# A two-layer hybrid encoder on one core: the mixer's GpSimd sums taken off GpSimd, the score scale moved from bias to q, and the v loads spread

## The chip, the core and the metric

The kernel runs on one core of one Trainium2 chip. TensorE (PE in the profile) multiplies, VectorE (DVE), ScalarE (ACT) and GpSimd (POOL) work on tiles in SBUF, and SyncE (SP) issues most of the transfers. The metric is the time of one execution in microseconds on the device. Lower is better.

## What is computed

```python
for l in range(2):
    x = x + 0.5 * swiglu(rms_norm(x, ffn1_norm[l]), ffn1_w_in[l], ffn1_w_out[l])
    x = x + mixer(rms_norm(x, mix_norm[l]), ...)
    x = x + 0.5 * swiglu(rms_norm(x, ffn2_norm[l]), ffn2_w_in[l], ffn2_w_out[l])
return rms_norm(x, final_norm)

def mixer(h, w_in, gate_bias, rpb, w_na_out, w_f_out, w_o):
    z = h @ w_in                       # q, k, v (512 each), uf (512), ga, gf (1024 each)
    y_na = neighbourhood_attention(q, k, v, rpb) @ w_na_out   # scores * 64**-0.5 + bias, softmax
    y_f = fourier_mix(uf) @ w_f_out    # real part of a 2-D DFT over positions and channels
    return (sigmoid(ga + gate_bias[0]) * y_na + sigmoid(gf + gate_bias[1]) * y_f) @ w_o
```

There are 512 positions of 1024 features in float32, 8 heads of 64, an 8 by 64 grid, and a feed-forward width of 2816.

## The kernel before

Each matrix is used as a sum of two parts, a rounded high part and the remainder, so every product takes three matmuls: high by high, high by low, low by high (`mm3`, L326 to L328; `product_T`, L515 to L517). The large products are done by a seven-product scheme on 2 by 2 blocks; its steps are numbered 1 to 7, and some take sums of weight blocks and sums of activation blocks.

All weights come through one stream, `ws`, a fixed list of items in the order of use. An item's raw tile is loaded by SyncE (L152). `high` makes `whi` on ScalarE (L186, L184 with a sign change) and `low` makes `wlo` on VectorE (L193, L191). `ws.next` prepares up to two items ahead. Sums of two weight blocks are made in two ways: by an accumulating transfer that GpSimd issues onto the raw tile (L154 when it is loaded, L203 after its low part is taken), or, for an item with `op=ALU.subtract`, by loading both blocks and a GpSimd subtraction (L166).

```python
            if self.add:
                self.add.load()
                if self.op is not ALU.add:
                    G.tensor_tensor(self.raw.t, self.raw.t, self.add.t, self.op)
```

`stage_mixer` writes out the order of its work by hand; each engine runs its own queue in order, and the scheduler keeps that order except for small moves. In order of time it does:

- `proj_V`: the v projection for four row blocks, and the even (`hp`, from `plus`) and odd (`hm`) combinations of the normalised rows for the Fourier branch. The odd one is a GpSimd subtraction (L1004). v goes to a DRAM tensor `vd` by SyncE (L974).
- `proj_U`: the Fourier input by even weights (`ue`, items "up") and odd weights (`uo`, items "um" less "un", L166).
- 14 loads of `vc` from `vd` (seven tiles, two halves each, L1410), all issued by SyncE right after `proj_U`.
- `proj_q`, `proj_k` for four head pairs, eight `att_step`s (scores, transposes and the product with `vc` are pipelined over three steps), and the position and channel transforms between them. `bias_for` loads the bias tiles `bm`; GpSimd multiplies them by 8 (L1169), and the scores take the bias with a factor of 1/8 for the whole sum (L1192).
- `f_fill`: the Fourier output rows in eight parts, with even (`pe`, items "fp" plus "fq") and odd (`po`, items "fp" less "fq", L166) products in two PSUM banks each.
- `gate_block` 0 and 1: the two gate projections by the seven products, tiles A, B and C, with sums of activation blocks made by `minus` on VectorE (`t1`) and GpSimd (`t3`, L1469, L1471) and by `fourth` on GpSimd (L1476, L1477). Between them `fill_n` multiplies the attention output by its weights.
- the output projection `w`, and the next stage's norm.

All tiles named "k" share 23 buffers of 4 KB per partition; PSUM has 8 banks used in turn.

Of the kernel before, what the change touches and what calls it, by code (L numbers as in the profile page):

```python
# [9 lines left out]
F32 = mybir.dt.float32  # L10
F32R = mybir.dt.float32r
# [83 lines left out]
def encoder_kernel(  # L95
# [60 lines left out]
    class Item:  # L156
        def __init__(self, raw, add=None, neg=False, stage=0, parts=1, pieces=1, then=None, op=ALU.add, kept=False):
            self.raw, self.add, self.neg, self.stage, self.parts = raw, add, neg, stage, parts
            self.pieces, self.then, self.op, self.kept = pieces, then, op, kept

        def load(self):
            self.raw.load(self.pieces)
            if self.add:
                self.add.load()
                if self.op is not ALU.add:
                    G.tensor_tensor(self.raw.t, self.raw.t, self.add.t, self.op)  # L166

        def high(self):
            n = self.raw.n
            if self.kept:  # L170
                self.out = (slot(F32R, "whi", (1024,))[:, 0:n], slot(F32R, "wlo", (1024,))[:, 0:n])
            else:
                self.out = tuple(
                    wp.tile([P, 1024], F32R, tag=z, name=nm(z), bufs=3)[:, 0:n] for z in ("whi", "wlo")
                )
            t = self.raw.t
            if self.add and self.op is ALU.add:
# [27 lines left out]
    def stage_items():  # L205
# [46 lines left out]
        for l in range(L):  # L252
# [8 lines left out]
            for g in range(2):  # L261
                add(Raw((s, "um", g)), Raw((s, "un", g)), op=ALU.subtract)
            for g in range(8):
                add(Raw((s, "qk", g)))
            for i in range(2):
                add(Raw((s, "fp", i), 1024, (s, "fq", i)))
                add(Raw((s, "fp", i)), Raw((s, "fq", i)), op=ALU.subtract)
            for i in range(2):
                strassen(s, lambda q: "g" + q, i, two, ORDER_0[0 : 2 - i], True)
            for g in range(2):  # L270
                add(Raw((s, "n", 0, g)))
            for i, order in ((0, (5,)), (1, (2,)), (0, (6, 7, 3, 4)), (1, (5, 6, 7, 3, 4))):
                strassen(s, lambda q: "g" + q, i, two, order, True)
                st += not i and len(order) == 1
            for g in range(2):
# [5 lines left out]
    class Stream:  # L281
# [5 lines left out]
        def fetch(self, to):  # L287
            n = len(self.items)
            while self.loaded < min(to, n) and self.items[self.loaded].stage <= self.stage:
                self.items[self.loaded].load()  # L290
                self.loaded += 1

        def high(self):
            self.fetch(self.highs + FETCH[self.stage % 2])
            self.items[self.highs].high()
            self.highs += 1
# [627 lines left out]
    def stage_mixer(l, norm, nxt):  # L924
# [29 lines left out]
        def proj_V():  # L954
# [45 lines left out]
            def plus(i):  # L1000
                a, b, t = norm.raw[i, 0], norm.raw[i, 1], folds[i]
                V.tensor_tensor(t[:, :, 1:HALF], a[:, :, 1:HALF], b[:, :, HALF - 1 : 0 : -1], ALU.add)
# [37 lines left out]
            ws.low()  # L1040
            h0, h1 = upper(norm.raw[0, 0], "hm"), upper(norm.raw[1, 0], "hm")
            for c in (0, 1):
                done(c, True)
            for c in (0, 1):
                done(c, False)
            hm.append(lower(h0, norm.raw[0, 0], "hm"))
            hm.append(lower(h1, norm.raw[1, 0], "hm"))

# [123 lines left out]
        def att_scores(i, after):  # L1172
            hp, pr = divmod(i, 2)
# [17 lines left out]
            for e, jj, c, z in quarters:  # L1191
                V.tensor_tensor_reduce(  # L1192
                    s_[e][:, c], ps[e][:, c], bms[hp][e][:, pr + jj, :], -(DH**-0.5), 3.0e38, ALU.add, ALU.min,
                    nmx[:, z : z + 1],
# [3 lines left out]
            for e, jj, c, z in quarters:  # L1198
# [3 lines left out]
                if jj:  # L1202
                    V.reciprocal(rs[:, 2 * e : 2 * e + 2], sm[:, 2 * e : 2 * e + 2])
            se = s_[0].rearrange("p (a k) -> p a k", a=2)
            V.tensor_tensor(se, se, rs[:, 0:2].unsqueeze(2).to_broadcast([P, 2, 256]), ALU.mult)
# [41 lines left out]

        def att_step(i, then=None, before=None, last=None):
            if 0 <= i - 2 < 8:
# [7 lines left out]
            if i < 8:  # L1257
                sc[i] = att_scores(i, last)

# [15 lines left out]
        def f_fill(w64):  # L1275

            for i in range(2):
                (eh, el), (oh, ol) = ws.next(0), ws.next(0)
                for cb in range(4):
                    if cb % 2 == 0:  # L1280
                        fs[i, cb // 2] = slot(F32, "fs", (2, T))
                    pe, po = bank(), bank()
                    for gp in range(2):
                        c = slice(gp * T + cb * P, gp * T + cb * P + P)
                        mm3(pe[:, 0:KC], eh[:, c], el[:, c], pf[gp][:, 0, :], pf[gp][:, 1, :], gp == 0, False)
                    c = slice(i * T + cb * P, i * T + cb * P + P)
                    PE.matmul(pe[:, 0:KC], w64[0:68, c], p64[0][0:68, 0:KC], start=False, stop=True)
                    for gp in range(2):
                        c = slice(gp * T + cb * P, gp * T + cb * P + P)
                        mm3(po[:, 0:HALF], oh[:, c], ol[:, c], qf[gp][:, 0, :], qf[gp][:, 1, :], gp == 0, gp == 1)  # L1290
                    t = tmp(s="fo")[:, 0:HALF]
                    S.activation(t, po[:, 0:HALF], AF.Copy)
                    y = fs[i, cb // 2][:, cb % 2, :]
                    S.activation(y[:, HALF : HALF + 1], pe[:, HALF : HALF + 1], AF.Copy)
                    V.tensor_tensor(y[:, 0:HALF], pe[:, 0:HALF], t, ALU.subtract)
                    V.tensor_tensor(y[:, T - 1 : HALF : -1], pe[:, 1:HALF], t[:, 1:HALF], ALU.add)
# [105 lines left out]
        vch = {}  # L1402
        for b in range(7):
            t = vch[b] = slot(F32R, "vc", (2, T))
            for z in range(2):
                src = bass.AP(
                    tensor=vd.tensor, offset=vd.offset + (b + z) * 8 * 2 * T,
                    ap=[[GW * 2 * T, ROWS], [2 * T, 8], [1, 2 * T]],
                )
                nc.sync.dma_start(out=t[64 * z : 64 * z + 64].bitcast(F32), in_=src.bitcast(F32))  # L1410
# [17 lines left out]
        bias_for(3)  # L1428
        att_step(4)
        proj_k(3)  # L1430
        ws.prep(ws.pos + 2)
        att_step(5, lambda: ws.prep(ws.pos + 3))
        f_rows = f_fill(w64)
# [3 lines left out]
        block_1 = gate_block(1, acts, ORDER_0, {}, ga1, gf1, (1, 2))  # L1437
        for _ in range(4):
            next(f_rows)
        ws.high()  # L1440
        att_step(6, ws.low)
        ws.prep(ws.pos + 3)
        for _ in range(4):
            next(f_rows)
# [49 lines left out]
        next(block)  # L1494
        *_, t3 = third
        next(block_1)
# [14 lines left out]
        ws.high()  # L1511
        h3 = high(t3, "t3")
        ws.low()
        acts[7] = low(h3, t3, "t3")
        next(block)
        next(block)
        ws.high()
        next(block)
        ws.low()
        next(block)  # L1520
        ws.high()
        next(block_1)
        ws.low()
        ws.high()
        next(block_1)
        ws.low()
        ws.high()
        next(block_1)
        next(block)
# [8 lines left out]
        written.pop().__exit__(None, None, None)  # L1538
        for _ in block:
            pass  # L1540

        m00, m01 = ga0
# [259 lines left out]
```

## Time and profile before

| | |
|---|---|
| three runs | 1938.55, 1940.87, 1946.59 us; median 1940.87 us |
| the profiled execution | 1944.28 us; its span is 1942.5 us |
| mean granted TensorE clock | 0.989 |
| busy: PE, PE weight load, DVE, ACT, POOL | 97%, 82%, 78%, 60%, 14% |
| moved | 378.91 MB, mean 195 GB/s |

The first mixer lies about between 300 and 612 us of the span, the second between 1264 and 1572 us. TensorE's order of work is fixed, so the profile is read as a list of places where TensorE waits; for each, the engine that ended the wait is followed back. The granted clock in the windows tells how fast TensorE ran after a wait.

### The profile page before, as it was taken

How to read it: one execution, taken by the hardware profiler on the slowest of the kernel's cores; microseconds unless marked ns; L12 is line 12 of the kernel's file. 1: busy time of each engine (PE TensorE's matmuls, PEld its weight loads, DVE VectorE, ACT ScalarE, POOL GpSimd, SP SyncE). 2: the span in 40 equal slices, each digit the busy share in tenths (PEclk: the TensorE clock that was granted, in tenths of full speed). 3: DMA queues.
4: the chain of work that ended last, by engine and by line, in shares of the span. 5: the costliest groups of instructions: out<-in, count | busy, mean ns of one | idle time of the engine just before them, and what ended most of it. 6: DMA issues, size and time to landing. Idle time of an engine off the chain costs nothing.

```text
span 1942.5 us, 25866 instructions
## 1 busy us (share of the span) xinstructions
PE 1886.3 (97%) x9609; PEld 1595.9 (82%) x9609; DVE 1520.5 (78%) x1864; ACT 1157.3 (60%) x1718; POOL 263.8 (14%) x242
## 2 busy tenths in 40 slices
PE   9999999989899999999999999999998999999997
PEld 7888888878898888888888888888798978888886
DVE  7777799748768866779976768997586787777898
ACT  6655666547555755566655556665575666556664
POOL 0101011311411000101000100123213110000010
PEclk9999999999999999999999999999999999999998
DMA  8776497673877467749847665967639774765593
GB/s 284 204 205 187 150 257 248 205 182 120 221 189 202 132 188 201 192 151 253 248 142 199 193 178 168 264 202 245 178 130 230 194 194 127 208 180 172 173 281 125
DMA packets 108301, 378.91 MB, mean 195 GB/s; under 512 B 12288, under 2 KB 12416, under 8 KB 108176
## 3 DMA queue, kind: packets, MB, share of 16 engines
q1 hardware_dynamic: 80096, 279.38, 40.2%
q0 software_dynamic: 27648, 97.59, 27.0%
q8 instruction: 75, 1.23, 0.2%
q14 instruction: 50, 0.41, 0.1%
q10 hardware_dynamic: 432, 0.30, 0.1%
HBM read 370.93 MB, written 6.29 MB: 194 GB/s over the span
## 4 chain that ended last, share of the span: by engine, by line
PE 64%; DVE 17%; DMA 7%; issue 5%; ACT 5%; SPq 1%; POOL 0%; DVEq 0%; ACTq 0%; POOLq 0%
PE A L326 7%; PE A L328 7%; PE A L327 7%; DMA raw<-in_wst_dram 5%; DVE wlo L193 5%; PE B L328 4%; PE B L326 4%; PE B L327 4%; PE o L327 3%; PE o L328 3%; PE o L326 3%; PE C L327 2%; PE C L328 2%; PE C L326 2%; PE tr L558 2%
## 5 line engine op out<-in xcount | busy, mean ns | idle before, releaser
L193 DVE TENSOR_TENSOR wlo<-raw,whi 128x1024 fp32r<-128x1024 f32 (+2 forms) x524 | 631.2, 1213 | 319.2 <-ACT whi L186 315.7
L186 ACT ACTIVATE whi<-raw 128x1024 fp32r<-128x1024 f32 (+2 forms) x524 | 539.0, 1034 | 468.0 <-PE A L328 116.3
L154 POOL DMA_DIRECT2D raw<-in_wst_dram x162 | 142.5, 896 | 1383.9 <-DMA raw<-in_wst_dram 894.1
L178 DVE TENSOR_TENSOR raw<-raw,raw 128x1024 f32<-128x1024 f32 (+1 forms) x128 | 151.1, 1191 | 2.5
L328 PE MATMUL A<-whi,xl 128*128 128x512 f32 x320 | 124.6, 389 | 0.0
L326 PE MATMUL A<-whi,xh 128*128 128x512 f32 x320 | 124.5, 389 | 0.0
L327 PE MATMUL A<-wlo,xh 128*128 128x512 f32 x320 | 124.5, 389 | 0.0
L184 ACT ACTIVATE whi<-raw 128x1024 fp32r<-128x1024 f32 x76 | 79.2, 1042 | 67.8 <-PE B L328 33.2
L191 DVE SCALAR_TENSOR_TENSOR wlo<-raw,whi 128x1024 fp32r<-128x1024 f32 x76 | 96.1, 1269 | 20.0 <-ACT whi L184 19.9
L535 ACT ACTIVATE sn<-A 128x512 f32<-128x512 f32 x96 | 56.5, 598 | 40.3 <-PE A L328 40.1
L327 PEld LDWEIGHTS A<-wlo,xh 128*128 128x128 f32 x320 | 60.1, 188 | 12.5
L328 PEld LDWEIGHTS A<-whi,xl 128*128 128x128 f32 x320 | 60.1, 188 | 12.4
L326 PEld LDWEIGHTS A<-whi,xh 128*128 128x128 f32 x320 | 60.1, 188 | 12.4
L326 PE MATMUL B<-whi,t1h 128*128 128x512 f32 x160 | 63.7, 398 | 0.0
L327 PE MATMUL C<-wlo,xh 128*128 128x512 f32 x160 | 62.4, 390 | 0.5 <-DVE wlo L193 0.5
L327 PE MATMUL A<-wlo,t2h 128*128 128x512 f32 x160 | 62.4, 390 | 0.4 <-DVE wlo L193 0.4
L326 PE MATMUL A<-whi,t3h 128*128 128x512 f32 x160 | 62.4, 390 | 0.2 <-ACT sn L535 0.2
L326 PE MATMUL C<-whi,xh 128*128 128x512 f32 x160 | 62.2, 390 | 0.2 <-ACT whi L186 0.2
L328 PE MATMUL B<-whi,t1l 128*128 128x512 f32 x160 | 62.4, 390 | 0.0
L327 PE MATMUL A<-wlo,t3h 128*128 128x512 f32 x160 | 62.3, 390 | 0.0
L328 PE MATMUL A<-whi,t2l 128*128 128x512 f32 x160 | 62.3, 389 | 0.0
L327 PE MATMUL B<-wlo,t1h 128*128 128x512 f32 x160 | 62.3, 389 | 0.0
(426 smaller groups left out, 5339.4 us busy)
## 6 DMA issues: line engine op xcount, KB each, us to landing
raw<-in_wst_dram SPq DMA_DIRECT2D x467, 512.0 KB
raw<-in_wst_dram POOLq DMA_DIRECT2D x172, 512.0 KB, 7.9
raw<-in_wst_dram SPq DMA_DIRECT2D x30, 256.0 KB
vc<-vd SPq DMA_DIRECT2D x28, 256.0 KB
bm<-in_near_dram SPq DMA_DIRECT2D x16, 384.0 KB
vd<-v SPq DMA_DIRECT2D x8, 512.0 KB
dft<-in_dft_dram POOLq DMA_DIRECT2D x4, 514.0 KB, 8.3
x<-in_xin_dram SPq DMA_DIRECT2D x4, 512.0 KB
```

Of the source, the lines that this page charges most:

```text
L154: G.dma_start(out=self.t, in_=wst[GRAN_AT[self.plus]][:, 0 : self.n], accum_op=ALU.add)
L178: V.tensor_tensor(t, t, self.add.t, ALU.add)
L184: S.activation(self.out[0][:, cs], self.raw.t[:, cs], AF.Copy, scale=-1.0)
L186: S.activation(self.out[0][:, cs], self.raw.t[:, cs], AF.Copy)
L191: self.last = V.scalar_tensor_tensor(lo, t, -1.0, hi.bitcast(F32), ALU.mult, ALU.subtract)
L193: self.last = V.tensor_tensor(lo, t, hi.bitcast(F32), ALU.subtract)
L326: PE.matmul(ps, lh, rh, start=start, stop=False, skip_group_check=again)
L327: PE.matmul(ps, lh, rl, start=False, stop=False, skip_group_check=again)
L328: PE.matmul(ps, ll, rh, start=False, stop=stop, skip_group_check=again)
L535: S.activation(t[:, b, :], ps[b], AF.Copy)
L558: PE.transpose(tr[:, k, b * P : (b + 1) * P], a[:, b, (q + k) * P : (q + k + 1) * P], ident)
```

## The change

- The four subtracted weight items of each layer ("um" less "un" twice, "fp" less "fq" twice) are loaded as one block, negated in place by ScalarE (`ws.negate`), and the other block is added by an accumulating transfer that GpSimd issues.
- The odd combination of rows (`less_mirror`), the block sums of `t3` and those of `fourth` are made by VectorE.
- q is scaled by 1/8 when it is split into its two parts, the low part in four pieces; the bias is used as it is loaded.
- The 14 loads of `vc` are issued in four groups (`keys`), after k 0, after q 1, after the channel transform and after k 1.
- The even and odd products of `f_fill` share one PSUM bank per part, and the first part of each four is emptied in the middle of an `att_step` (`mid`).
- Step 5 of gate block 1 is put ahead of step 4 of gate block 0, in the weight stream and on TensorE.

The diff, cut to its core:

```diff
+        def negate(self):
+            t = self.raw.t
+            S.activation(t, t, AF.Copy, scale=-1.0)
+            G.dma_start(out=t, in_=wst[GRAN_AT[self.minus]][:, 0 : self.raw.n], accum_op=ALU.add)
+            self.minus = None
...
-                add(Raw((s, "um", g)), Raw((s, "un", g)), op=ALU.subtract)
+                add(Raw((s, "un", g)), minus=(s, "um", g))
...
-                add(Raw((s, "fp", i)), Raw((s, "fq", i)), op=ALU.subtract)
+                add(Raw((s, "fq", i)), minus=(s, "fp", i))
...
-            for i, order in ((0, (5,)), (1, (2,)), (0, (6, 7, 3, 4)), (1, (5, 6, 7, 3, 4))):
+            for i, order in ((0, (5,)), (1, (2,)), (0, (6, 7, 3)), (1, (5,)), (0, (4,)), (1, (6, 7, 3, 4))):
...
-                G.tensor_tensor(a[:, :, 1:HALF], a[:, :, 1:HALF], b[:, :, HALF - 1 : 0 : -1], ALU.subtract)
+            def less_mirror(i):
+                a, b = norm.raw[i, 0], norm.raw[i, 1]
+                V.tensor_tensor(a[:, :, 1:HALF], a[:, :, 1:HALF], b[:, :, HALF - 1 : 0 : -1], ALU.subtract)
...
             ws.high()
+            ws.negate()
             some((0, 1), VG[2], False, False)
+            ws.low()
             hp.append(lower(h1, folds[1], "hp"))
-            ws.low()
+            less_mirror(0)
             ws.high()
+            ws.negate()
...
-            split(hv, lv, proj_T().rearrange("p (r j c) -> p j r c", r=ROWS, j=4))
+            ps = proj_T().rearrange("p (r j c) -> p j r c", r=ROWS, j=4)
+            S.activation(hv, ps, AF.Copy, scale=DH**-0.5)
+            for j in range(4):
+                V.scalar_tensor_tensor(
+                    lv[:, j], ps[:, j], DH**-0.5, hv[:, j].bitcast(F32), ALU.mult, ALU.subtract
+                )
...
-                G.tensor_single_scalar(res, res, DH**0.5, ALU.mult)
...
-                    pe, po = bank(), bank()
+                    ps = bank("ef")
+                    pe, po = ps[:, 0:KC], ps[:, HALF:]
...
+        def keys(*bs):
+            for b in bs:
...
         proj_k(0)
+        keys(0, 1)
         proj_q(1)
+        keys(2, 3)
         att_step(0)
         four_ch()
         bias_for(1)
+        keys(4)
         proj_k(1)
+        keys(5, 6)
...
+        ws.negate()
+        att_step(4, lambda: ws.prep(ws.pos + 2))
+        ws.negate()
+        ws.prep(ws.pos + 3)
         proj_k(3)
...
-        first, third = minus(V, B[0, 0], B[0, 1], "t1"), minus(G, B[0, 1], B[1, 1], "t3")
+        first, third = minus(V, B[0, 0], B[0, 1], "t1"), minus(V, B[0, 1], B[1, 1], "t3")
         def fourth():
-            G.tensor_tensor(t12, B[1, 0][0], t12, ALU.subtract)
-            G.tensor_tensor(t12, t12, B[1, 0][1], ALU.add)
+            V.tensor_tensor(t12, B[1, 0][0], t12, ALU.subtract)
+            V.tensor_tensor(t12, t12, B[1, 0][1], ALU.add)
```

More of the change, by code (lines that the diff above doesn't have):

```diff
@@ L291, in fetch, with negate @@
                 self.loaded += 1
+        def negate(self):
+            next(z for z in self.items[self.highs :] if z.minus).negate()
         def high(self):
             self.fetch(self.highs + FETCH[self.stage % 2])
+            assert self.items[self.highs].minus is None
             self.items[self.highs].high()
@@ L1203, in att_scores @@
                     V.reciprocal(rs[:, 2 * e : 2 * e + 2], sm[:, 2 * e : 2 * e + 2])
+                    if mid and not e:
+                        mid()
             se = s_[0].rearrange("p (a k) -> p a k", a=2)
@@ L1246, in stage_mixer, with att_step @@
         sc, pt_ = {}, {}
-        def att_step(i, then=None, before=None, last=None):
+        def att_step(i, then=None, before=None, last=None, mid=None):
             if 0 <= i - 2 < 8:
@@ L1257, in att_step @@
             if i < 8:
-                sc[i] = att_scores(i, last)
+                sc[i] = att_scores(i, last, mid)
         fs, ns = {}, {}
@@ L1437, in stage_mixer @@
         block_1 = gate_block(1, acts, ORDER_0, {}, ga1, gf1, (1, 2))
-        for _ in range(4):
+        ws.high()
+        att_step(5, ws.low, mid=lambda: next(f_rows))
+        for _ in range(3):
             next(f_rows)
         ws.high()
-        att_step(6, ws.low)
-        ws.prep(ws.pos + 3)
-        for _ in range(4):
+        att_step(6, ws.low, mid=lambda: next(f_rows))
+        ws.prep(ws.pos + 1)
+        for _ in range(3):
             next(f_rows)
@@ L1511, in stage_mixer @@
         ws.high()
-        h3 = high(t3, "t3")
         ws.low()
-        acts[7] = low(h3, t3, "t3")
+        next(third)
         next(block)
         next(block)
+        next(third)
         ws.high()
@@ L1519, in stage_mixer @@
         ws.low()
+        t3 = next(third)
         next(block)
         ws.high()
+        h3 = high(t3, "t3")
         next(block_1)
@@ L1527, in stage_mixer @@
         ws.high()
+        acts[7] = low(h3, t3, "t3")
         next(block_1)
@@ L1538, in stage_mixer @@
         written.pop().__exit__(None, None, None)
-        for _ in block:
-            pass
+        for _ in range(2):
+            next(block)
+        next(block_1)
+        next(block)
         m00, m01 = ga0
```

57 lines of the change are left out of this document (28 added, 29 removed).

## The prediction, made before the changed kernel was run

> **What bounds the kernel now.** I read the page's busy times first, then the list of waits for TensorE, then the timeline around each long wait on all engines, and last the windows with the granted clock.
>
> ```profile
> PE 1886.3 (97%) x9609; PEld 1595.9 (82%) x9609; DVE 1520.5 (78%) x1864; ACT 1157.3 (60%) x1718; POOL 263.8 (14%) x242
> ...
> PE A L517 <- DVE wlo L191: 10.4, 2, 5.2
> PE ps L326 <- DVE q L333: 9.1, 2, 6.5
> ...
> PE B L515 <- ACT whi L186: 3.3, 2, 1.7
> PE ps L326 <- ACT fs L1294: 3.2, 4, 0.9
> ...
> PE ue L327 <- DVE wlo L193: 2.9, 2, 2.5
> PE uo L327 <- DVE wlo L193: 2.5, 2, 2.4
> PE B L517 <- DVE wlo L193: 1.5, 2, 0.8
> ```
>
> TensorE is the bound at 97%, and the change leaves its instructions as they are in number (on the queues of the built kernels only one product changes its place). So the time can fall only by what TensorE waits, and by the slow clock behind a wait. The rows give total, times and longest. They all lie in the two mixers, nearly each once in either.
>
> The clock behind three of these waits, in each layer:
>
> ```profile
> 412.90:420.20 7.30, 7.29 (x25) 5.79 (x26) 4.98 (x17) 5.78 (x17) 3.32 (x2) 0.75 0.79 215
> 503.20:508.70 5.50, 5.48 (x24) 5.38 (x25) 5.46 (x8) 3.20 (x6) 1.48 (x2) 0.50 1.07 264
> 548.70:552.80 4.10, 4.10 (x22) 4.10 (x23) 4.10 (x6) 2.66 (x5) 0.00 (x0) 0.61 0.60 187
> 1373.00:1381.40 8.40, 8.36 (x24) 6.63 (x25) 5.86 (x17) 5.78 (x17) 3.31 (x2) 0.64 0.65 170
> 1464.30:1468.60 4.30, 4.24 (x22) 4.24 (x23) 4.25 (x8) 2.66 (x5) 0.64 (x1) 0.60 1.07 276
> 1509.10:1513.20 4.10, 4.10 (x23) 4.10 (x24) 4.10 (x6) 2.65 (x5) 0.00 (x0) 0.62 0.51 191
> ```
>
> Third from the end stands the granted clock. Length times what is missing to 1: behind the q wait 7.30 x 0.25 + 8.40 x 0.36 = 4.8 us; behind the A wait 5.50 x 0.50 + 4.30 x 0.40 = 4.5 us; behind the B waits 4.10 x 0.39 + 4.10 x 0.38 = 3.2 us. That is time beside the waits themselves.
>
> The Trainium skill (TensorE: Matmul & The Clock Gate, Part 1) says that the clock halves only after an idle window of about 3.4 us. By that rule only the waits of 6.5 and 5.2 us would have a slow tail, 3.0 us less would come back than I count, and the forecast below would be 1912.5. The rows differ: the B waits (1.7 us and under) and the second q wait (9.1 - 6.5 = 2.6 us) also have one. The measurement decides.
>
> **Part 1, v loads.**
>
> ```profile
> 375.46 15.63 SPq L1410 DMA_DIRECT2D vc<-vd  x14
> 392.23 20.39 SPq L152 DMA_DIRECT2D raw<-in_wst_dram  x7
> 409.95 1.06 ACT L186 ACTIVATE whi<-raw 128x1024 fp32r<-128x1024 f32 x1 [12.65 <-DMA raw<-in_wst_dram]
> 412.18 0.68 DVE L333 TENSOR_TENSOR q<-ps,q 128x512 fp32r<-128x512 f32 x1
> 412.92 0.80 PE L326 MATMUL ps<-xh,whi 128*128 128x512 f32 x1 [6.50 <-DVE q L333]
> 427.63 0.28 PE L326 MATMUL ps<-p,vc 128*128 128x256 f32 x1
> ```
>
> The wait named "q" is a late weight: 14 loads of `vc` stand on SyncE's queue before the next raw block, which lands at 409.95; ScalarE and VectorE hold the q split behind that block's whi and wlo, and TensorE needs the split's PSUM bank. In the built kernel's SyncE queue three weight blocks (qk 4 to 6) move ahead of all `vc` loads, and qk 7 and the first f block go between them. So this wait goes, 9.1 us, with its tail of 4.8: 13.9 us. What is moved late is `vc`, first read at 427.63. All 14 and the block behind them took 409.95 - 375.46 = 34.5 us; with three blocks first (SyncE spent 20.39 / 7 = 2.9 us on one) the first eight of 14 land near 375.5 + 9 + 34.5 x 8/14 = 404, an estimate, and even a first read 8.3 us (6.5 + 1.8) earlier leaves 15 us. Cost: nothing; if buffers hold the loads back by more than those 15 us, part 1 is lost, which is a rival below.
>
> **Part 2, GpSimd sums.**
>
> ```profile
> 493.39 2.48 DVE L1469 TENSOR_TENSOR t<-xl 128x1024 f32<-128x1024 f32 x1
> 494.75 3.38 POOL L1469 TENSOR_TENSOR t<-xl,xl 128x1024 f32<-128x1024 f32 x1
> 495.91 3.31 DVE L1471 TENSOR_TENSOR t<-t,t 128x1024 f32<-128x1024 f32 x1
> 497.75 0.28 PE L516 MATMUL A<-xl,whi 128*128 128x256 f32 x1
> 499.14 4.03 DVE L191 SCALAR_TENSOR_TENSOR wlo<-raw,whi 128x1024 fp32r<-128x1024 f32 x1
> 499.43 2.65 POOL L1471 TENSOR_TENSOR t<-t,t 128x1024 f32<-128x1024 f32 x1
> ...
> L193 DVE TENSOR_TENSOR wlo<-raw,whi 128x1024 fp32r<-128x1024 f32 (+2 forms) x524 | 631.2, 1213 | 319.2 <-ACT whi L186 315.7
> ...
> L333 DVE TENSOR_TENSOR xl<-xr,xh 128x1024 fp32r<-128x1024 f32 x16 | 19.6, 1223 | 4.9 <-ACT xh L332 4.5
> L1002 DVE TENSOR_TENSOR ht<-xr,xr 128x1020 f32<-128x1020 f32 x4 | 4.8, 1210 | 0.0
> L333 DVE TENSOR_TENSOR q<-ps,q 128x512 fp32r<-128x512 f32 x8 | 5.5, 686 | 1.7 <-ACT q L332 1.7
> L1192 DVE CUSTOM_DVE_ANT_0 s<-ps,bm 128x256 f32<-128x256 f32 x64 | 23.2, 419 | 0.0
> ```
>
> A VectorE operation on two SBUF blocks of 128x1024 takes 1.22 us; the three beside GpSimd's sums take 2.48, 3.31 and 4.03. At 1.22 each the wlo that TensorE waits for ends 6.2 us sooner, at 497.0, ahead of the 497.9 where it is wanted. The A wait goes: 10.4 + 4.5 = 14.9 us.
>
> What VectorE takes over per layer: two mirrors, 2 x 1.21; three sums for t3, 3 x 1.22; two for fourth, 2 x 1.22; and four q splits in four pieces. A piece is 0.29 by the line through 0.686 (512) and 0.419 (256), so a split grows by 0.46, at most by 4 x 0.419 - 0.686 = 1.0. Together 2.4 + 3.7 + 2.4 + 1.8 = 10.4 us. I cost it at nothing: what hides it is VectorE's idle time ahead of wlo, 315.7 us in the run, and on its queue t3 and fourth stand after `fill_n` among such wlo; q is read two steps later. If that cover is gone, it is 20.8 us in all.
>
> One thing is late next: the second weight block of `fill_n`. On VectorE two operations of 512 columns, two of 256, and three of 1024 with its own wlo follow on 497.0: 2 x 0.69 + 2 x 0.42 + 3 x 1.22 = 5.9, so 502.9. TensorE ends A at 497.9 + 5.50 x 0.50 = 500.6 and wants that wlo eight matmuls later, at 0.23 each (7.30 x 0.75 over 24) 502.4. A wait of 0.5, 1.0 us for both layers, between none and 3.
>
> **Part 3, odd weights by negation.**
>
> ```profile
> 356.00 3.45 SPq L152 DMA_DIRECT2D raw<-in_wst_dram  x5
> 362.92 2.86 POOL L166 TENSOR_TENSOR raw<-raw,raw 128x1024 f32<-128x1024 f32 x1 [0.44 <-DMA raw<-in_wst_dram]
> 363.48 6.82 DVE L193 TENSOR_TENSOR wlo<-raw,whi 128x780 fp32r<-128x780 f32 x3
> 366.66 0.39 PE L327 MATMUL ue<-wlo,hph 128*128 128x260 f32 x1 [2.50 <-DVE wlo L193]
> 374.51 0.28 PE L326 MATMUL uo<-whi,hmh 128*128 128x256 f32 x1
> 447.15 1.06 ACT L1273 ACTIVATE w<-r 4x1024 fp32r<-4x1024 f32 x1
> 458.53 0.28 PE L326 MATMUL ps<-pq,whi 128*128 128x256 f32 x1
> ...
> DMA to landing us min/median/max: 5.1/7.9/13.9
> ```
>
> The ue and uo waits, 2.9 + 2.5 = 5.4 us, come from wlo operations of 6.82 / 3 us beside L1004 and L166; without GpSimd the even weights are ready in time. But a chain takes the subtraction's place: load, negate (1.06), an accumulating transfer, whi (1.06), wlo (1.22). For uo: the block lands one SyncE issue (0.69) earlier than the pair at 362.92, so 362.2; negated 363.2; with a landing L later, hi and lo are ready at 365.5 + L. ue takes 374.51 - 366.66 = 7.85 us, so uo wants its low part at 366.66 - 2.50 - 0.28 + 7.85 + 0.12 = 371.9 (0.28 is the matmul before the wait, 0.12 the step from one to the next: 5.50 x 0.50 over 24). The new wait is L - 6.4: 1.5 us at the median of 7.9. For f_fill: the negation follows the copy that ends at 448.2, so it ends at 449.3; hi and lo are ready at 451.6 + L, and TensorE wants them at 458.5: L - 6.9, 1.0 us. Of both, 2.5 us a layer, 5.0 in all; at 5.1 nothing; at 13.9 7.2 us each and a slow clock. ScalarE's queue holds the next whi, the mirror's high part and the v copies behind the negation's wait for its load; they have over a microsecond. The four transfers stand on POOL's queue where it had waited for the sums. The bias scaling leaves GpSimd and no one waited for it.
>
> **Part 4, one bank, and the order of steps.** Four parts of two banks took all 8 banks, and TensorE waited for them: 3.2 us, gone. Step 5 ahead of step 4 gives block 1's transfers more room; the two loads it moves past are ahead anyway. I cost it at nothing. The B waits stay:
>
> ```profile
> 546.32 2.00 ACT L186 ACTIVATE whi<-raw 128x1024 fp32r<-128x1024 f32 x2 [5.40 <-DMA raw<-in_wst_dram]
> ```
>
> They end on a crowded accumulating transfer that the change does not touch, 3.3 + 1.5 us with 3.2 of clock: 8.0 us, at best also gone.
>
> **Sum.** 13.9 + 14.9 + 5.4 + 3.2 = 37.4 us gone; 1.0 + 5.0 us new; net 31.4. The profiled execution took 1944.28 us (span 1942.5), 0.2% over the median of the runs, 1940.87. Against its own time: 1912.9; against the median, which I forecast: **1909.5 us**.
>
> **Rivals.** *VectorE becomes the bound* (0.15): at 78% it takes 20.8 us more, all of it on the path: net 10.6, 1930.3 us. For it: its rows above follow each other without a gap from 493.39 to 503.17. Against: three of its operations there get 6.2 us back. The Trainium skill (Perfetto Trace Analysis, Optimizing Scalar/DVE Operations) speaks on this side: with VectorE saturated, handing work to GpSimd may pay; it adds that the two share a read port. The rows above bear out the second half.
>
> *The v loads only move the crowd* (0.08): another weight is late by as much, part 1 gives nothing: net 17.5, 1923.4 us. Against: the SyncE queue as built.
>
> *The sums were not what slowed VectorE* (0.07): then A, ue and uo waits stay: 37.4 - 14.9 - 5.4 = 17.1, less 3.0: 1926.8 us. Against: three slow operations, each beside a GpSimd sum.
>
> *Slower: the negation chain* (0.06): both places of a layer cost L - 6.65 and a slow clock of some 2.3 us (9.3 / 4). The gain without it, 36.4, is used up, and 9.7 us (0.5%, about what a measurement here can tell) more, when 4 x (L - 4.35) = 46.1, so from L = 15.9 us. At 17: 1940.87 - 36.4 + 50.6 = 1955 us. For it: 13.9 is the longest in this mixer. Against: the median, 7.9.
>
> **How the numbers follow.** The forecast has 0.62, and 0.02 is left for others. Low end: no chain cost and the B waits gone, 1940.87 - 37.4 - 8.0 = 1895. High end: past the VectorE rival, 1932. Faster by over 0.5% is below 1931.2: the forecast and nearly all of the first three rivals, 0.88; same 0.06, slower 0.06.
>
> **Right or wrong.** Right: TensorE's waits on q, on A's L191 and on fs are gone from the list; the windows behind them show clock 1.00; VectorE's 128x1024 operations are all near 1.22; uo and f_fill wait 1 to 2 us; the B waits stay near 4.8. Wrong: a wait of TensorE on `vc`, on a whi held by a transfer behind a negation, or on a wlo behind the new sums.

## The result

Two sets of runs agree. In the first the changed kernel's median is 1918.38 us (1917.10 to 1922.43) against 1940.47 us (1938.55 to 1946.59) before, a ratio of 0.988, 95% interval 0.986 to 0.991. In the second it is 1920.50 us (1915.30 to 1924.81) against 1938.78 us, ratio 0.992, 0.988 to 0.995. It is faster by about 1%; forecast were 1909.5 us and a range of 1895 to 1932, so the time lies in the range and 8.9 us above the forecast.

The first profile's span is 1917.7 us, 24.8 under that of before. Its busy times, and then its list of waits, less those of stages that the change does not touch:

```profile
PE 1879.4 (98%) x9609; PEld 1590.5 (83%) x9609; DVE 1507.6 (79%) x1902; ACT 1166.5 (61%) x1726; POOL 176.4 (9%) x212
```
```profile
...
PE ef L336 <- DVE wlo L197: 3.5, 2, 1.7
PE B L523 <- ACT whi L190: 3.2, 2, 1.9
...
PE ps L1239 <- DVE s L1227: 2.6, 4, 1.1
PE uo L335 <- DVE wlo L197: 1.8, 2, 0.9
PE uo L334 <- ACT whi L190: 1.7, 2, 1.1
PE B L525 <- DVE wlo L197: 1.5, 2, 0.8
PE ps L336 <- DVE wlo L197: 0.8, 2, 0.4
```

The waits on q (9.1), on A's L191 (10.4), of ue (2.9) and for the bank of fs (3.2) are gone, and the one announced in `fill_n` is there (L336, 0.8 in all). The B waits stand. New and larger than forecast are the waits inside `f_fill`: ef on a low part, 3.5, and the transposes (L1239) on the scores s, 2.6. VectorE has 38 instructions more and is 12.9 us less busy, and none of its operations takes longer than 1.3 us, where 20 of the kernel before took 1.5 to 4.0. In the windows of the changed kernel, columns as before (third from the end the granted clock), the first two are behind the old q wait, the next two behind the old A wait, the last behind the B waits:

```profile
404.00:410.40 6.40, 6.40 (x34) 5.29 (x32) 3.83 (x9) 4.43 (x11) 0.96 (x1) 1.00 0.67 164
1356.20:1362.60 6.40, 6.40 (x35) 5.24 (x34) 3.83 (x8) 4.52 (x11) 0.96 (x1) 1.00 0.39 79
485.40:491.20 5.80, 5.80 (x50) 5.80 (x50) 5.72 (x9) 4.19 (x8) 3.48 (x4) 1.00 1.01 367
1437.50:1443.30 5.80, 5.80 (x50) 5.80 (x50) 5.72 (x9) 4.19 (x8) 3.44 (x4) 1.00 1.05 405
532.60:537.50 4.90, 4.86 (x22) 4.86 (x23) 4.90 (x7) 2.66 (x5) 0.86 (x1) 0.50 0.54 130
```

The clock is 1.00 where it had been 0.75, 0.64, 0.50 and 0.60, and 0.50 still behind the B waits.

For all kernels together, TensorE's timeline is cut where it starts a new step: U from the first ue product to the first q product; v from the channel transform to the scores of attention step 1, which holds the q wait; f from the first product of `f_fill` to the first of A; A to `fill_n`; `fill_n` to B; B to the output projection. Each number is the length in the profiled execution, both layers added, less that of before, in us. The medians are of 4 to 10 runs, taken on several chips; the kernel before has medians of 1938.8 to 1943.7 beside them, so a few us between two medians settle little. A "+" before a kernel's name marks an edit of the changed kernel, "before" one of the kernel before.

| kernel | U | v | f | A to n | n to B | B to w | median of runs | profiled run |
|---|---|---|---|---|---|---|---|---|
| forecast | -2.4 | -13.9 | -1.2 | -14.9 | +1.0 | 0 | 1909.5 | |
| changed | -0.2 | -14.2 | +2.2 | -13.8 | +1.1 | +1.3 | 1918.4 | 1919.5 |
| changed, again | -4.2 | -14.2 | +5.2 | -14.5 | -0.3 | +0.5 | 1920.5 | 1918.3 |
| before, v loads spread | +0.8 | -14.2 | +0.1 | -0.5 | -0.3 | +2.0 | 1933.1 | 1934.0 |
| + v loads together | -3.4 | +8.0 | +3.7 | -14.2 | +0.4 | +2.1 | 1931.6 | 1945.0 |
| before, sums on VectorE | +1.7 | -11.4 | +1.2 | -14.5 | +0.6 | +2.9 | 1928.7 | 1925.3 |
| before, GpSimd writes for t3 | 0.0 | -1.2 | +0.3 | -14.5 | +0.6 | +9.6 | 1937.7 | 1943.3 |
| before, and for fourth | 0.0 | -5.6 | +0.3 | -14.5 | +0.6 | +3.1 | 1930.8 | 1928.5 |
| + negations in idle time | -3.9 | -14.2 | -1.6 | -13.8 | +1.2 | 0.0 | 1911.7 | 1914.7 |
| + rows not in a step | -3.7 | -14.2 | +3.9 | -10.3 | +6.4 | -5.4 | 1924.3 | 1924.4 |
| + GpSimd subtraction | +1.0 | -14.2 | -1.7 | -13.8 | +1.2 | -0.9 | 1918.2 | 1916.4 |
| + step 5 ahead of step 3 | -3.5 | -14.2 | +5.2 | -14.5 | -0.3 | -8.7 | 1908.8 | 1909.0 |
| + three repairs | -4.2 | -14.2 | -4.7 | -13.1 | +1.1 | -8.7 | 1900.8 | 1900.8 |
| + four repairs | -4.0 | -14.2 | -4.7 | -13.1 | +1.1 | -8.7 | 1904.1 | 1904.2 |

### The profile page after: what moved, and what is told of

Read it like the earlier page. It is cut to its first block, busy times and chain, and to the rows that moved or that the text cites. A ratio compares the mean times of both kernels' runs of the same rounds, so it can differ in the third digit from the quotient of the medians.

```text
span 1917.7 us, 25845 instructions
## 1 busy us (share of the span) xinstructions
PE 1879.4 (98%) x9609; PEld 1590.5 (83%) x9609; DVE 1507.6 (79%) x1902; ACT 1166.5 (61%) x1726; POOL 176.4 (9%) x212
## 3 DMA queue, kind: packets, MB, share of 16 engines
q8 instruction: 75, 1.23, 0.3%
## 4 chain that ended last, share of the span: by engine, by line
PE 73%; DVE 15%; issue 5%; ACT 4%; DMA 3%; POOL 0%; ACTq 0%; SPq 0%; DVEq 0%; POOLq 0%
PE A L334 7%; PE A L336 7%; PE A L335 7%; DVE wlo L197 5%; PE B L334 4%; PE B L336 4%; PE B L335 4%; PE o L335 3%; DMA raw<-in_wst_dram 3%; PE o L336 3%; PE o L334 3%; PE ps L334 2%; PE ps L336 2%; PE ps L335 2%; PE C L335 2%
## 5 line engine op out<-in xcount | busy, mean ns | idle before, releaser
L197 DVE TENSOR_TENSOR wlo<-raw,whi 128x1024 fp32r<-128x1024 f32 (+2 forms) x524 | 620.0, 1190 | 300.8 <-ACT whi L190 297.4
L336 PE MATMUL A<-whi,xl 128*128 128x512 f32 x320 | 124.6, 389 | 0.0
L195 DVE SCALAR_TENSOR_TENSOR wlo<-raw,whi 128x1024 fp32r<-128x1024 f32 x76 | 90.5, 1195 | 20.0 <-ACT whi L188 19.8
L336 PEld LDWEIGHTS A<-whi,xl 128*128 128x128 f32 x320 | 60.1, 188 | 12.5
L336 PE MATMUL B<-whi,t1l 128*128 128x512 f32 x160 | 62.4, 390 | 0.0
L336 PE MATMUL A<-whi,t2l 128*128 128x512 f32 x160 | 62.3, 389 | 0.0
```

Source lines behind the costliest of these rows:

```text
L195: self.last = V.scalar_tensor_tensor(lo, t, -1.0, hi.bitcast(F32), ALU.mult, ALU.subtract)
L197: self.last = V.tensor_tensor(lo, t, hi.bitcast(F32), ALU.subtract)
L336: PE.matmul(ps, ll, rh, start=False, stop=stop, skip_group_check=again)
```

## The experiments

**The v loads, done alone and undone.** First the kernel before with the four groups of `keys`, then the changed kernel with all 14 loads behind `proj_U`.

```diff
...
         proj_k(0)
+        keys(0, 1)
         proj_q(1)
+        keys(2, 3)
...
+        keys(4)
         proj_k(1)
+        keys(5, 6)
```

> The kernel before, with the 14 loads of vc in four groups and nothing else changed. Theory (the loads stand in the way of the next weight block): TensorE's wait of 9.1 us on q goes, the two windows behind it run at clock 1.00 in place of 0.75 and 0.64, and no wait on vc appears: 13 to 15 us less than the kernel before, about 1926.5. Rival (the crowd only moves: another weight is late by as much): a new wait of 5 us or more of TensorE between k 1 and the first f block, and a time within 4 us of the kernel before, about 1938.

> The changed kernel, with the 14 loads of vc issued together behind the U stage again. Theory: the wait on q comes back with 8 to 10 us in the run and with its slow clock: 13 to 15 us over the changed kernel, about 1932.5. Rival (with GpSimd free the weight queue has more room, so that the loads no longer matter): under 4 us over the changed kernel.

Spread alone: 1933.09 us, ratio 0.996, 0.995 to 0.998. In its list of waits q and `vc` do not occur, and A's wait stays:

```profile
PE A L517 <- DVE wlo L191: 9.3, 2, 4.8
PE ue L327 <- DVE wlo L193: 5.1, 2, 2.6
```

The v stretch is 14.2 us shorter, as the theory said, but the median falls by 7.1. Undone: 1931.60 us, 11 to 13 over the changed kernel, but from 1926.36 to 1944.97. The profiled run is the slowest of these, and its waits and whi rows show why:

```profile
PE ps L334 <- DVE q L1175: 17.6, 2, 10.6
```
```profile
409.90 1.06 ACT L190 ACTIVATE whi<-raw 128x1024 fp32r<-128x1024 f32 x1 [12.93 <-DMA raw<-in_wst_dram]
1374.35 1.06 ACT L190 ACTIVATE whi<-raw 128x1024 fp32r<-128x1024 f32 x1 [16.43 <-DMA raw<-in_wst_dram]
```

The weight behind the loads lands late by a varying amount: in the ten places of the five profiles of kernels with the loads together, its whi starts 29.4 to 36.2 us after the first of the 14 loads is issued. The v stretch of these is 22.3, 28.0, 32.4, 33.6 and 41.6 us, both layers added, with the slow clock behind the waits in it; in all nine with the loads spread it is 19.5. The five differ in other edits too, and what sets the landing was not tried. So the 9.1 us of the forecast were one draw. The edit also seems to narrow the runs: beside each other on one chip, the kernel before went from 1934.2 to 1949.9 us (20 runs), the changed kernel with the loads together from 1926.4 to 1945.0 (10 runs), the one before with spread loads from 1929.8 to 1934.0 (5 runs).

**GpSimd's sums on VectorE, alone.** The kernel before; t3 and fourth only, at the changed kernel's places.

```diff
-        first, third = minus(V, B[0, 0], B[0, 1], "t1"), minus(G, B[0, 1], B[1, 1], "t3")
+        first, third = minus(V, B[0, 0], B[0, 1], "t1"), minus(V, B[0, 1], B[1, 1], "t3")
         def fourth():
-            G.tensor_tensor(t12, B[1, 0][0], t12, ALU.subtract)
-            G.tensor_tensor(t12, t12, B[1, 0][1], ALU.add)
+            V.tensor_tensor(t12, B[1, 0][0], t12, ALU.subtract)
+            V.tensor_tensor(t12, t12, B[1, 0][1], ALU.add)
...
```

> The kernel before, with only the sums of t3 and fourth moved from GpSimd to VectorE, at the changed kernel's places; the mirror of the rows and the subtracted weights stay on GpSimd. Theory (VectorE ran slowly beside GpSimd's sums): the wait of 10.4 us of A on wlo goes and the clock behind it is 1.00, the waits of ue and uo stay (5.4 us), a wait of some 0.4 us per layer comes in fill_n: 13 to 15 us less, about 1926.5. Rival (VectorE becomes the bound, 2 x 5 operations of 1.22 us on the path): 12 us back, so within 4 us of the kernel before.

1928.66 us, ratio 0.995, 0.993 to 0.996. A to n is 14.5 us shorter and n to B 0.6 longer: the step gains what it should. The median falls by 11.5 us, less than the 13 to 15 expected; in the profile B to w gives 2.9 us back. (Its v stretch happens to be a short draw.)

**What slows VectorE.** The kernel before; first GpSimd's three operations for t3 are replaced by zero writes into the same tiles, then also the two for fourth, so the result is left without t3 and then without fourth too.

```diff
+        def cleared(s):
+            t = [slot(F32, s), slot(F32, s)]
+            for z in range(2):
+                G.memset(t[z], 0.0)
+                yield t[z]
+            G.memset(t[0], 0.0)
+            yield t[0]
+
-        first, third = minus(V, B[0, 0], B[0, 1], "t1"), minus(G, B[0, 1], B[1, 1], "t3")
+        first, third = minus(V, B[0, 0], B[0, 1], "t1"), cleared("t3")
...
-            G.tensor_tensor(t12, B[1, 0][0], t12, ALU.subtract)
-            G.tensor_tensor(t12, t12, B[1, 0][1], ALU.add)
+            G.memset(t12, 0.0)
+            G.memset(t12, 0.0)
```

> The kernel before, with the three GpSimd operations that make t3 (two subtractions and an addition of 128x1024 blocks) replaced by three that only write zeros into the same tiles at the same places; so t3 is left out of the result, and GpSimd is as busy there as before or nearly. Theory (it is GpSimd's reading of two blocks that slows VectorE's reading of two blocks): the three VectorE operations of 2.48, 3.31 and 4.03 us take 1.22 each, the wait of 10.4 us goes, and the time is 13 to 15 us less, about 1926.5. Rival (any work of GpSimd on SBUF slows VectorE, or the wait has another cause): they stay over 2 us and the time stays near 1940.

> The kernel before, with GpSimd's three operations for t3 and its two for fourth replaced by operations that only write zeros into the same tiles (t3 and fourth are left out of the result). With only t3's replaced, two wlo operations beside fourth's sums took 7.21 us and TensorE waited 5.0 us for B. Theory (reading by both engines is what slows VectorE, and the second pair of sums had been hidden by the wait at the first): now neither wait is there, 13 to 15 us less than the kernel before, about 1926.5, some 10 us under the run with t3's alone. Rival (the B waits there come from a late transfer): the B wait of 2.4 us stays and the time is near 1937.

The first: 1937.68 us, ratio 0.998, 0.996 to 1.001: by its time no gain that can be told. By its timeline the theory holds twice, on GpSimd and VectorE of the first mixer:

```profile
496.42 0.96 POOL L1477 MEMSET t<- 128x1024 f32 x1 [0.57 <-PE ps L328]
...
495.93 1.21 DVE L1469 TENSOR_TENSOR t<-xl 128x1024 f32<-128x1024 f32 x1
497.17 1.23 DVE L1471 TENSOR_TENSOR t<-t,t 128x1024 f32<-128x1024 f32 x1
498.32 1.22 DVE L191 SCALAR_TENSOR_TENSOR wlo<-raw,whi 128x1024 fp32r<-128x1024 f32 x1
...
516.15 7.21 DVE L193 TENSOR_TENSOR wlo<-raw,whi 128x1024 fp32r<-128x1024 f32 x2 [2.80 <-ACT whi L186]
516.23 2.71 POOL L1484 TENSOR_TENSOR t<-xh,t 128x1024 f32<-128x1024 f32 x1
519.01 3.26 POOL L1485 TENSOR_TENSOR t<-t,xl 128x1024 f32<-128x1024 f32 x1
520.08 0.39 PE L517 MATMUL B<-t1h,wlo 128*128 128x256 f32 x1 [2.44 <-DVE wlo L193]
```

The three operations that had taken 2.48, 3.31 and 4.03 us take 1.21 to 1.23, one of them beside a zero write, and A's wait is gone (-14.5). But TensorE's work now comes earlier against GpSimd's, and fourth's sums, which read, fall on two low parts: 7.21 us for two, and TensorE waits 2.44 us for the second. In the kernel before these low parts came 1.9 us after fourth's sums had ended (516.74 + 2.40 = 519.14):

```profile
516.74 2.40 POOL L1477 TENSOR_TENSOR t<-t,xl 128x1024 f32<-128x1024 f32 x1
...
521.06 2.36 DVE L193 TENSOR_TENSOR wlo<-raw,whi 128x1024 fp32r<-128x1024 f32 x2 [7.65 <-ACT whi L186]
```

So 9.6 us are given back from B on: the B waits on wlo grow from 1.5 to 5.0 us, those on whi from 3.3 to 4.9, and where the other 4.5 us go was not traced. With both replaced: 1930.81 us, ratio 0.994, 0.992 to 0.995; B to w falls from +9.6 to +3.1. The zero writes are also shorter than the sums (0.95 to 1.28 us against 2.4 to 3.4), so part of the difference may be that they are over sooner; the one that lay beside a zero write (496.42 to 497.38) ran at full speed all the same and ended before it, at 497.14. The rows also show how the slow ones are slow. Each ends 1.09 us after the sum beside it: the sums end at 498.13, 502.08 and 522.27 (494.75 + 3.38, 499.43 + 2.65, 519.01 + 3.26), the VectorE operations at 499.22, 503.17 and 523.36. That is about the time of one operation, so they look held until the sum is over rather than slowed all along; no run tests this by itself. The Trainium skill (SBUF — State Buffer, Who interferes with whom) says that a VectorE instruction with two SBUF inputs contends with a GpSimd instruction that reads SBUF, and not with one that only writes; both halves agree with these rows, 3.6 us (7.21 / 2) against 1.21. And moving the sums to VectorE costs what leaving them out costs: -14.5, +0.6 and +2.9 against -14.5, +0.6 and +3.1. VectorE's idle time did hide them.

**The waits in `f_fill`.** The changed kernel, three ways. First, both negations are put where ScalarE waits for row minima.

```diff
-        att_step(3)
+        att_step(3, last=ws.negate)
...
-        ws.negate()
-        att_step(4, lambda: ws.prep(ws.pos + 2))
-        ws.negate()
+        att_step(4, lambda: ws.prep(ws.pos + 2), last=ws.negate)
```

> The changed kernel, with the two negations for f_fill moved on ScalarE's queue into the 1.47 us in which it waits for the row minima of attention steps 3 and 4 (both blocks have landed by then). Theory (the 6.1 us of waits in f_fill, 3.5 of ef on wlo and 2.6 of the transposes on s, come from the 2.1 us that the negations add to ScalarE's queue ahead of the first odd whi, not from the transfers): the odd whi stands 1.8 us earlier against the start of f_fill, the two waits shrink to 1 to 3 us in the run, and the time is 3 to 5 us under the changed kernel's 1918.4, about 1914.5. Rival (the transfer behind the negation is what is late): a whi of f_fill that waits for DMA, the same waits. Rival (the row emptied in the middle of a step is the cause): the wait of 1.12 on s stays twice.

1911.72 us, ratio 0.985, 0.981 to 0.988: 7 to 9 us under the two medians of the changed kernel, where 3 to 5 were expected. ScalarE and TensorE in the changed kernel, first mixer, where `f_fill` starts at 446.89:

```profile
444.97 1.04 ACT L168 ACTIVATE raw<-raw 128x1024 f32<-128x1024 f32 x1
445.92 1.04 ACT L190 ACTIVATE whi<-raw 128x1024 fp32r<-128x1024 f32 x1
456.22 1.06 PE L1239 MATMUL ps<-ident,s 128*128 128x128 f32 x8 [1.12 <-DVE s L1227]
461.20 0.38 PE L336 MATMUL ef<-pq,wlo 128*128 128x256 f32 x1 [1.73 <-DVE wlo L197]
```

and with the negations moved, where it starts at 449.02, with VectorE ahead of the wait:

```profile
446.15 1.04 ACT L190 ACTIVATE whi<-raw 128x1024 fp32r<-128x1024 f32 x1
...
457.51 1.10 ACT L190 ACTIVATE whi<-raw 128x1024 fp32r<-128x1024 f32 x1
...
458.69 0.41 DVE L1323 TENSOR_TENSOR fs<-ef,fo 128x255 f32<-128x255 f32 x1
459.27 0.86 DVE L1266 TENSOR_TENSOR o<-ps,o 64x256 fp32r<-64x256 f32 x2 [0.17 <-ACT o L1263]
460.16 1.22 DVE L197 TENSOR_TENSOR wlo<-raw,whi 128x1024 fp32r<-128x1024 f32 x1
461.44 0.38 PE L336 MATMUL ef<-pq,wlo 128*128 128x256 f32 x1 [1.42 <-DVE wlo L197]
```

The first whi (a row without a DMA wait: its block was there) stands 2.9 us ahead of `f_fill` in place of 1.0. The wait on s falls to 0.3 in all, that on wlo only to 2.8. So the queue of ScalarE was the cause of the one, and not, or little, of the other.

Second, the rows are emptied after the attention step.

```diff
-        att_step(5, ws.low, mid=lambda: next(f_rows))
-        for _ in range(3):
+        att_step(5, ws.low)
+        for _ in range(4):
...
```

> The changed kernel, with the first part of each four of f_fill emptied after the attention step again, not in its middle. Theory (negations): the waits of ef on wlo stay near 3.5, the wait on s falls by the 0.5 to 0.75 us of work that stood ahead of it in either layer, and the time changes by under 2 us. Rival (the middle of the step is the cause): both waits go, 6 us, about 1912.5.

1924.34 us, ratio 0.991, 0.987 to 0.994. That is 4 to 6 us over the two medians of the changed kernel, where under 2 were expected, but the runs overlap (1922.0 to 1925.3 against 1915.3 to 1924.8) and the ratios do not differ. The ef wait stays at 3.4, that on s falls to 1.6, and later low parts are late: waits of 3.2 us on A's and 2.5, from 0.8, on those of `fill_n`, while B to w is 6 us shorter than in the changed kernel. So emptying a row inside the step did not cause the ef wait; whether it pays is not settled.

Third, the subtraction goes back to GpSimd, with both blocks loaded.

```diff
-                add(Raw((s, "un", g)), minus=(s, "um", g))
+                add(Raw((s, "um", g)), less=Raw((s, "un", g)))
...
+            if self.less:
+                self.less.load()
+                G.tensor_tensor(self.raw.t, self.raw.t, self.less.t, ALU.subtract)
...
```

> The changed kernel, with the four odd weight items of a layer loaded as two blocks and subtracted by GpSimd again, in place of the negation and the accumulating transfer; the sums of activations stay on VectorE. Theory (the subtraction slows VectorE beside it, the negation takes ScalarE's time): the wait of ue on wlo comes back with 3 to 5 us, those of uo (1.8 us and more) go, the wait of the transposes on s (2.6 us) goes, the wait of ef on wlo stays near 2.8; so within 3 us of the changed kernel's 1918.4. Rival (the negation is a plain loss): no wait of ue, 5 us or more under the changed kernel. Rival (it is a plain gain, as predicted): 3 us or more over it.

1918.20 us, ratio 0.988, 0.985 to 0.990: the same time as the changed kernel. The reason is not all as expected: ue does not wait, but uo does, for both parts.

```profile
PE uo L337 <- ACT whi L193: 2.8, 2, 1.4
PE ef L339 <- DVE wlo L200: 2.8, 2, 1.4
PE uo L338 <- DVE wlo L200: 2.6, 2, 1.3
```

`f_fill` is as short as with the negations in idle time (-1.7 and -1.6), so the negations on ScalarE's queue cost there 3.8 us against the changed kernel's first profile. In U the negation is the better way (-4.2 to -3.4 in seven of the eight profiles with it, -0.2 in the eighth, +1.0 here). The two cancel.

**The B waits.** Step 5 of gate block 1 is put ahead of step 3 of block 0.

```diff
-            for i, order in ((0, (5,)), (1, (2,)), (0, (6, 7, 3)), (1, (5,)), (0, (4,)), (1, (6, 7, 3, 4))):
+            for i, order in ((0, (5,)), (1, (2,)), (0, (6, 7)), (1, (5,)), (0, (3, 4)), (1, (6, 7, 3, 4))):
...
-        for _ in range(2):
-            next(block)
+        next(block)
         next(block_1)
-        next(block)
+        for _ in range(2):
+            next(block)
```

> The changed kernel, with step 5 of gate block 1 ahead of step 3 of block 0, in the weight stream and on TensorE. Theory (step 3 waits for an accumulating transfer that is issued at the end of step 6, with only step 7 between, and lands 13 us later beside the loads for block 1): 5.8 us more room; the B waits of 4.7 us and the slow clock behind them (about 4 us) go: 6 to 9 us under the changed kernel, about 1911. Rival (the transfers of block 1 that now come earlier are as late): a wait of 2 us or more in block 1's step 5 or 6, and a time within 3 us of 1918.4.

1908.75 us, ratio 0.983, 0.980 to 0.986. No wait of B is left in the list, and B to w is 8.7 us under before, 9 to 10 under the changed kernel. The second transfer for step 3 and the whi that needs it, in the changed kernel and with the new order:

```profile
516.83 1.22 POOL L207 DMA_DIRECT2D raw<-in_wst_dram  x1
...
530.27 2.00 ACT L190 ACTIVATE whi<-raw 128x1024 fp32r<-128x1024 f32 x2 [5.36 <-DMA raw<-in_wst_dram]
```
```profile
518.12 1.22 POOL L207 DMA_DIRECT2D raw<-in_wst_dram  x1
...
532.34 1.06 ACT L190 ACTIVATE whi<-raw 128x1024 fp32r<-128x1024 f32 x1 [2.19 <-DMA raw<-in_wst_dram]
```

It takes as long as before from issue to whi, 14.2 us against 13.4. It is not faster, only wanted later.

**The repairs together.** Negations in idle time, step 5 ahead, and the second odd block of `f_fill` in tiles of its own, split ahead of the rows; then, as a fourth (the last added line), also the loads of the odd U blocks ahead of two writes of v.

```diff
-                add(Raw((s, "fq", i)), minus=(s, "fp", i))
+                add(Raw((s, "fq", i)), minus=(s, "fp", i), kept=i == 1)
...
-        att_step(5, ws.low, mid=lambda: next(f_rows))
+        att_step(5, ws.low, last=ws.high, mid=lambda: next(f_rows))
+        ws.low()
         for _ in range(3):
             next(f_rows)
-        ws.high()
-        att_step(6, ws.low, mid=lambda: next(f_rows))
+        att_step(6, mid=lambda: next(f_rows))
...
+            ws.fetch(ws.highs + 5)
             done(2, True)
```

> The changed kernel with three repairs: the negations in ScalarE's idle time, step 5 of block 1 ahead of step 3 of block 0, and the second odd block of f_fill in tiles of its own, so that its high part is made while ScalarE waits for the row minima of step 5 and its low part ahead of the rows' evacuation on VectorE. The first two alone gave 1911.7 and 1908.75 us; if they add, 1902. Theory (the wait of ef that was left, 1.4 us in either layer, is the low part standing behind six row operations and two of o on VectorE): it goes, so 1899, between 1897 and 1903. Rival (its transfer then lands too late, or the rows' banks come free later): a wait of ef on whi or on fs of 1 us or more, 1902 or over.

> The kernel with three repairs, and the loads of both odd U blocks issued ahead of the two writes of v that SyncE had to wait for. Theory (the chain of load, negation and transfer ends the waits of uo, and starts with a late load): the uo waits of 1.6 to 1.8 us in the run go, 2 us under the run with three repairs, about 1897. Rival (the transfers, 8 us from issue, are as late as before because they then collide with the loads of the even blocks): the same waits, the same time within 1 us, or a wait of ue on whi in their place.

Three: 1900.76 us, ratio 0.979, 0.977 to 0.981, the fastest of all, 18 to 20 us under the changed kernel. The ef wait is gone (f -4.7 against -1.6 with the negations alone). So it came from splitting the second odd block behind the rows. The rows of the kernel with the negations moved point at VectorE: the high part ends at 458.61 (457.51 + 1.10), the low part starts at 460.16, behind the last row and o. But the repair moves both parts, so their shares were not separated. Four: 1904.05 us, ratio 0.980, 0.978 to 0.982: nothing gained, and 3.3 us over the run with three. The stages of the table are alike in both (-43.8 and -43.5 us in all); the loss lies outside them, where waits of the feed-forward product o on wlo are 6.1 us in place of 4.5 (3.7 to 6.7 in the other profiles), and what sets them was not tried. The uo waits stay at 1.8. Negation, issue and whi of the first odd block, with three and with four:

```profile
361.26 1.06 ACT L168 ACTIVATE raw<-raw 128x1024 f32<-128x1024 f32 x1 [1.70 <-DMA raw<-in_wst_dram]
362.62 0.88 POOL L169 DMA_DIRECT2D raw<-in_wst_dram  x1 [20.97 <-ACT raw L168]
370.29 1.06 ACT L190 ACTIVATE whi<-raw 128x1024 fp32r<-128x1024 f32 x1 [1.43 <-DMA raw<-in_wst_dram]
```
```profile
361.27 1.04 ACT L168 ACTIVATE raw<-raw 128x1024 f32<-128x1024 f32 x1
362.61 0.88 POOL L169 DMA_DIRECT2D raw<-in_wst_dram  x1 [18.90 <-ACT raw L168]
372.35 1.06 ACT L190 ACTIVATE whi<-raw 128x1024 fp32r<-128x1024 f32 x1 [3.02 <-DMA raw<-in_wst_dram]
```

The first ue product starts at 363.69 in the one and at 365.50 in the other, so against TensorE's work the transfer is issued 1.8 us earlier; it takes 9.7 us in place of 7.7 and lands where it did. That bears out the rival, as far as the landing; what it collides with was not separated.

**The changed kernel again**, for a second profile.

> The changed kernel once more, unaltered, for a second profile of it. In its first profile the U stages (first ue product to first q product, both layers) took 33.5 us, in five other kernels with the same U code 29.5 to 30.4. Theory (the landing of the odd blocks in that one profile was late): 29.5 to 30.5 us here, f_fill 45 to 49 us, v stretch 19.5 us, and 1913 to 1919. Rival (it is the changed kernel's own order of work that makes the U stage slow): 33 us again, and 1917 to 1920.

1920.50 us, over the 1913 to 1919 expected. U is 29.5 us, so the 33.5 of the first profile were not the order of work: there the transfer of the first odd block took 8.6 us to its landing in the second mixer, here 7.3, and uo waited for whi, here not. `f_fill` is at the long end, 48.8, as below. The wait in `fill_n` is not there.

## Why the prediction was right, and where not

*Part 1* held in its mechanism: forecast 13.9, in the profile 14.2. That the numbers meet is because both count from the same profile of the kernel before. What it did not say is that its 9.1 us of wait are one draw of a stretch that varies by 19 us; against the median the edit alone is worth 7.1.

*Part 2* held: forecast 14.9, measured 13.8 and 14.5. The mechanism was tested by the zero writes, and the cover on VectorE by the pair of runs that cost the same. The rival with VectorE as the bound is excluded. The announced wait of 0.5 us in each `fill_n` was 0.4 in the first profile and absent in the second.

*Part 3* failed for `f_fill`, and this is the main miss. The step "so it ends at 449.3; hi and lo are ready at 451.6 + L" took the landing as the only thing behind the negation. No whi there waited for DMA. What the negations cost is their own time on ScalarE's queue, one of them right ahead of the whi: 3.8 us where 2.0 was forecast for landings, and 6.8 in the second profile, with a slow clock behind the waits. For U the forecast was -5.4 + 3.0 = -2.4, the profiles show -0.2 and -4.2; the chain ends by landing there, as it said (7.7 us from issue to whi in the rows above, where L was taken as 7.9).

*Part 4* was right for the B waits, forecast 4.8 to stay, measured 4.7. It failed in "3.2 us, gone": it named nothing that is late next. The second odd block's low part is 1.4 us late in either layer; with its split ahead of the rows f falls by another 3.1.

*The sum.* In the first profile f is 3.4 us over the forecast, U 2.2, A to n 1.1 and B to w 1.3; with the small terms the steps give -23.6 where -31.4 was forecast, 7.8 short, and 1.2 came back outside them. The other 2.3 of the 8.9 are no cost of the change: the terms came from a profile 3.4 us over the median (1944.28 against 1940.87) and were taken from the median, and the profile after stands only 1.1 over its own. The change's parts were sized right where TensorE waited for one late thing, and too high in `f_fill`, where other work ended close behind the thing waited for.

The Trainium skill's rule on the clock (TensorE: Matmul & The Clock Gate, Part 1), halving only after an idle window of about 3.4 us, is not borne out as a threshold here: the B waits of 1.9 and 0.8 us have a window of 4.9 us at 0.50 behind them.

## What to carry to other kernels

When an operation moves to another engine, count its time on that engine's queue ahead of the next thing wanted there, not only its own chain; the cheap place is where that engine already waits. For each wait that goes, name what ends second there, and how much later it is allowed to be. Where a wait ends on a transfer that runs beside many others, one profile is one draw. Here an order that gave the transfer room was worth 9 to 10 us, and one that started it 1.8 us earlier nothing.

## What the runs showed of the hardware that was not expected

The same waits have a slow clock behind them in some executions and not in others. In `f_fill` the changed kernel waits 1.1 and 1.7 us in either profile. Windows from about the scores of attention step 6 to A, in the first profile and then in the second:

```profile
457.00:469.75 12.75, 11.02 (x100) 10.21 (x98) 10.65 (x29) 9.74 (x31) 0.00 (x0) 1.00 0.24 78
```
```profile
458.00:472.40 14.40, 12.67 (x99) 12.00 (x99) 12.25 (x34) 11.17 (x32) 0.00 (x0) 0.88 0.25 87
```

The clock is 1.00 and 0.88, which is 14.40 x 0.12 = 1.7 us. The second mixer shows the same (1.00 over 12.76 us, 0.88 over 14.30), so the clock accounts for the 3.0 us by which f differs between the two profiles. What decides it was not tried. The Trainium skill (TensorE: Matmul & The Clock Gate, Part 1) says that the window over which idleness is counted runs freely, whatever the kernel does; by that the same two waits could fall well or badly, which fits these rows and is not shown by them.

An accumulating transfer that was issued 1.8 us earlier, as TensorE's work goes, landed no earlier: 9.7 us to whi in place of 7.7, and in the second mixer the uo wait stayed at 0.9 too. Behind 14 loads of 256 KB on one queue the next block's whi starts 29.4 to 36.2 us after the first of them; with the waits and the slow clock that follow, the v stretch differs by 19 us between five kernels that issue the loads alike. And a VectorE operation on two SBUF blocks beside a GpSimd sum ends 1.09 us after the sum does.
